# A retention kernel's chunk loop: the normalisation of a chunk is queued ahead of the next chunk's operands, and sums of background products are made by accumulating DMAs

## The chip, the cores and the metric

The kernel runs on one core of one Trainium2 chip. The metric is the device time of one execution in microseconds (us), the median over several runs. An execution is also profiled once; the profile gives its span and what each engine did in it: TensorE (PE; its weight loads are PEld), VectorE (DVE), ScalarE (ACT), GpSimd (POOL) and SyncE (SP, which here only issues DMAs).

## The reference, cut to what matters

Two layers over 1024 tokens of width 1024. Layer 0 mixes tokens by retention, layer 1 by a state-space scan; each is followed by a gated MLP. The change touches the retention of layer 0 and the modulations, which are worked out in the background of that stage:

```
def step(state, qkv):                       # one chunk of 128 tokens, per head
    qc, kc, vc = qkv
    s = jnp.einsum('bhnd,bhmd->bhnm', qc, kc) * intra[None]
    o = (jnp.einsum('bhnm,bhmv->bhnv', s, vc)
         + jnp.einsum('bhnd,bhdv->bhnv', qc, state) * cross[None, :, :, None])
    state = (chunk_decay[None, :, None, None] * state
             + jnp.einsum('bhmd,bhmv->bhdv', kc * to_state[None, :, :, None], vc))
    return state, o
...
    mu = jnp.mean(o, axis=-1, keepdims=True)
    oc = o - mu
    o = oc * lax.rsqrt(jnp.mean(oc * oc, axis=-1, keepdims=True) + EPS)
...
    mod = cond @ ada_w[i] + ada_b[i]        # cond = silu(c), shift/scale/gate of both sub-layers
```

There are 4 heads with keys of 256 and values of 512, and 8 chunks of 128 tokens. `ada_w` is 2 x 1024 x 6144; ten of its twelve blocks of 1024 x 1024 are the background's.

## The kernel before, in words

**Products.** Every fp32 operand is split into a high and a low part, and a product is three matmuls into one PSUM bank (`mm3`, L822 to L825).

**The chunk loop.** The loop over heads (L1550) computes gates, q, k and the first value tiles, and then runs over 8 chunks. The program order of one turn `ci` is: `s2(ci)`, `s1(ci+1)`, `s2_norm`, `v_tile(ci+2)`, a tick, `s3(ci)`, a tick. Each engine runs its own instructions in this order.
- `s2(ci)` puts query x state (6 matmuls, from the second chunk on) and scores x values (3 matmuls) into the bank `ob`. DVE takes its mean and variance (bn_stats L1191, bn_aggr L1193) and adds epsilon (`gve`, L1195); POOL raises that to -1/2 (`grs`, L1197). Then 6 matmuls update the state, whose fp32 form `stf` and halves `sth`, `stl` come from DVE (L1208, L1213), ACT (L1209) and, for the second half, POOL (a tensor_tensor by the helper at L128).
- `s1(ci+1)` makes the next chunk's scores, masks them (`pf`, L1156) and splits them (`pp`, L1158, L1159), transposes and splits k (`kk`, L1167 on ACT, L1168 on DVE), and splits q (`qq`, L1172 on ACT, L1173 on DVE).
- `s2_norm` makes -mean x grs (`gnb`, L1221, DVE) and the normalised chunk `on` (L1222, ACT), which reads `ob`, `grs` and `gnb`.
- `v_tile(ci+2)` is 48 matmuls of 256 columns for a later chunk's values (L1133 to L1135). For the last two chunks a gate or output unit stands in its place.
- `s3(ci)` has four PE transposes of `on` (L1229), and DVE multiplies the gates `sg` by them (L1231). Every second chunk ACT issues a DMA of `sg` to `act_d`.

**The background.** A tick pumps the queue of weight loads and takes one step of the background queue. From the first heads on that is `ada_bg` (L547): 80 steps, ten sets of eight row blocks `kt`. A step issues on SP the load of the next 512 KB block into one of two buffers `ar` (L554), multiplies the present block by its column of `cond` on POOL (L513), and adds the product to the accumulator `aacc` on POOL (L515); for kt = 0 the multiplication writes `aacc` itself. After kt = 7, `ada_fold` transposes and reduces the accumulator on DVE, with the block's buffer as scratch (L522, L523). There is one accumulator. A turn of the chunk loop has two ticks, so two steps, and they stand on POOL between the `stl` of this chunk and the `grs` of the next. The steps run through the chunk loops of heads 0 to 2 (chunks 2 to 5 of head 0, 0 to 5 of heads 1 and 2, 16 turns with two steps each) and through the units between them.

**Accumulating DMAs.** A DMA that POOL issues with `accum_op` adds its source to its destination. In the kernel before only layer 1's MLP has them (L285, L286 and L288, 256 KB each, SBUF to SBUF).

Of the kernel before, what the change touches and what calls it, by code (L numbers as in the profile page):

```python
# [12 lines left out]
F32R = mybir.dt.float32r  # L13
I32 = mybir.dt.int32
AF = mybir.ActivationFunctionType
ALU = mybir.AluOpType
PSUM = bass.MemoryType.PSUM

P = 128
# [8 lines left out]
NCH = T // CH  # L28
# [53 lines left out]
def trunk_kernel(ctx: ExitStack, tc: tile.TileContext, x, c, pos, ada_w, ada_b, ret_w_in, ret_w_out,  # L82
# [13 lines left out]
    V = nc.vector  # L96
# [33 lines left out]
    def gp_ts(out, in0, c_):  # L130
        GP.tensor_scalar(out=out, in0=in0, scalar1=c_, scalar2=1.0, op0=ALU.mult, op1=ALU.mult)
# [4 lines left out]
    def f(ap):  # L136
        return ap.bitcast(F32)
# [372 lines left out]
    def ada_acc(eng, acc, raw, kt, first):  # L510
        o = acc if first else raw
        if first or eng is GP:
            eng.tensor_scalar(out=o, in0=raw, scalar1=cond[:, kt:kt + 1], scalar2=1.0, op0=ALU.mult, op1=ALU.mult)  # L513
            if not first:
                eng.tensor_tensor(out=acc, in0=acc, in1=raw, op=ALU.add)  # L515
        else:
            eng.scalar_tensor_tensor(out=acc, in0=raw, scalar=cond[:, kt:kt + 1], in1=acc, op0=ALU.mult, op1=ALU.add)  # L517
# [29 lines left out]
    def ada_bg(order, nb):  # L547
        seq = [(l, m, kt) for l, m in order for kt in range(8)]
        raws = {}

        def load(i):
            if i < len(seq):
                raws[i] = a_p.tile([P, D], F32, tag="ar", name="ar", bufs=2)
                SP.dma_start(out=raws[i], in_=ada_slab(*seq[i]))  # L554
        load(0)
        yield
        acc = None
        for i, (l, m, kt) in enumerate(seq):
            load(i + 1)
            if kt == 0:  # L560
                acc = a_p.tile([P, D], F32, tag="aacc", name="aacc")
            raw = raws.pop(i)
            ada_acc(GP, acc, raw, kt, kt == 0)
            yield
            if kt == 7:
                ada_fold(acc, raw, l, m)
        yield
        yield from ada_fin(nb())
# [575 lines left out]
    def s1(H, ci):  # L1144
        kt, qt = qk_chunk(H.k, ci), qk_chunk(H.q, ci)
        st = bank(B_S)
        for d in range(2):
            PE.matmul(st[:, 0:P], lhsT=kt[:, d, :], rhs=qt[:, d, :], start=(d == 0), stop=(d == 1))
        r = ci % 2
        if r == 0 or ci == 0:  # L1150
            H.pf = t_p.tile([P, 2, P], F32, tag="tE", name="pf")
            H.pp = t_p.tile([P, 2, 2, P], F32R, tag="tD", name="pp")
            H.kk = t_p.tile([P, 2, 2, 256], F32R, tag="tB", name="kk")
            H.qq = t_p.tile([P, 2, 2, 2, P], F32R, tag="tC", name="qq")
        pf = H.pf[:, r, :]
        V.tensor_tensor(out=pf, in0=st[:, 0:P], in1=cst[:, C_MASK + H.h * P:C_MASK + (H.h + 1) * P], op=ALU.mult)  # L1156
        ph, pl = H.pp[:, r, 0, :], H.pp[:, r, 1, :]
        V.tensor_copy(ph, pf)  # L1158
        V.tensor_tensor(out=pl, in0=pf, in1=f(ph), op=ALU.subtract)  # L1159
        H.P[ci] = (ph, pl)  # L1160
        if ci < NCH - 1:
            kb = bank(B_KT)
            for d in range(2):
                PE.transpose(kb[:, d * P:(d + 1) * P], kt[:, d, :], ident)
            sc = cst[:, C_KS + H.h:C_KS + H.h + 1]
            kh, kl = H.kk[:, r, 0, :], H.kk[:, r, 1, :]
            A.activation(out=kh, in_=kb[:, 0:256], func=AF.Copy, scale=sc)  # L1167
            V.scalar_tensor_tensor(out=kl, in0=kb[:, 0:256], scalar=sc, in1=f(kh), op0=ALU.mult, op1=ALU.subtract)  # L1168
            H.K[ci] = (kh, kl)
        if ci > 0:  # L1170
            qh, ql = H.qq[:, r, 0], H.qq[:, r, 1]
            A.activation(out=qh, in_=qt, func=AF.Copy)  # L1172
            V.tensor_tensor(out=ql, in0=qt, in1=f(qh), op=ALU.subtract)  # L1173
            H.Q[ci] = (qh, ql)

    def s2(H, ci):
        vt = H.v[ci]
        vh, vl = vt[:, 0:512], vt[:, 512:1024]
        ob = bank(B_O)
        if ci > 0:  # L1180
            qh, ql = H.Q.pop(ci)
            for d in range(2):
                sh_, sl_ = H.st[1][:, d * HW:(d + 1) * HW], H.st[2][:, d * HW:(d + 1) * HW]
                mm3(ob, qh[:, d, :], ql[:, d, :], sh_, sl_, d == 0, False)
        ph, pl = H.P.pop(ci)
        mm3(ob, ph, pl, vh, vl, ci == 0, True)
        r = ci % 2
        if r == 0:
            H.on = t_p.tile([P, 2, HW], F32, tag="tA", name="on")
        bs = s_p.tile([P, 6], F32, tag="bs", name="bs")  # L1190
        V.bn_stats(bs, ob)  # L1191
        mv = s_p.tile([P, 2], F32, tag="mv", name="mv")
        V.bn_aggr(mv, bs)  # L1193
        ve = s_p.tile([P, 1], F32, tag="gve", name="gve")
        V.tensor_tensor(out=ve, in0=mv[:, 1:2], in1=cst[:, C_EPS + H.h:C_EPS + H.h + 1], op=ALU.add)  # L1195
        rs = s_p.tile([P, 1], F32, tag="grs", name="grs")
        GP.tensor_tensor(out=rs, in0=ve, in1=mhalf[:, 0:1], op=ALU.pow)  # L1197
        if ci < NCH - 1:
            kh, kl = H.K.pop(ci)
            sc = float(np.exp(lg[H.h] * CH))  # L1200
            for d in range(2):
                sb = bank(B_ST[d])
                mm3(sb, kh[:, d * P:(d + 1) * P], kl[:, d * P:(d + 1) * P], vh, vl, True, True)
                sf, sh_, sl_ = (t[:, d * HW:(d + 1) * HW] for t in H.st)
                if ci == 0:
                    A.activation(out=sf, in_=sb, func=AF.Copy)
                else:
                    V.scalar_tensor_tensor(out=sf, in0=sf, scalar=sc, in1=sb, op0=ALU.mult, op1=ALU.add)  # L1208
                A.activation(out=sh_, in_=sf, func=AF.Copy)  # L1209
                if d:  # L1210
                    gp_tt(sl_, sf, f(sh_), ALU.subtract)
                else:
                    V.tensor_tensor(out=sl_, in0=sf, in1=f(sh_), op=ALU.subtract)  # L1213
        drop(H.v.pop(ci))
        H.n = (ci, ob, mv, rs)
# [334 lines left out]
    for h in range(HEADS):  # L1550
        if h == 1:
            bgq.insert(0, tables_in())
        while H.ng < 4:
            g_unit(H.h, H.ng, H.sg)
            H.ng += 1
        H.q = [take(F32, f"q{i}") for i in range(2)]
        for j in range(2):
            rot_unit("q", h, j, H.q)
        H.k = [take(F32, f"k{i}") for i in range(2)]
        for j in range(2):  # L1560
            rot_unit("k", h, j, H.k)
        H.wv = W.get(("v", h, 0, 0), 4)
        H.st = (take(F32, "stf"), take(F32R, "sth"), take(F32R, "stl"))
        v_tile(H, 0)
        tick()
        s1(H, 0)
        v_tile(H, 1)
        tick()
        N = late = None
        for ci in range(NCH):  # L1570
            s2(H, ci)
            if ci + 1 < NCH:
                s1(H, ci + 1)
            if late is not None:
                s3(H, late)
                late = None
            s2_norm(H)
            if ci + 2 < NCH:
                v_tile(H, ci + 2)
                tick()  # L1580
            elif h + 1 < HEADS:
                if N is None:
                    drop(*H.q, *H.k)
                    N = new_head(h + 1)
                g_unit(N.h, N.ng, N.sg)
                N.ng += 1
            else:
                RB = Rot([0, 1, 5]) if ci < NCH - 1 else RA
                ro_unit(act, 0, ci - (NCH - 2))
            if h == HEADS - 1 and ci == NCH - 6:  # L1590
                bg_drain()
                drop(cosT, sinT, H.q.pop(0), H.k.pop(0))
                act = []
                la = load_act(0, act)
            if h == HEADS - 1 and NCH - 6 <= ci < NCH - 3:
                next(la)
            if h == HEADS - 1 and ci == NCH - 3:
                for a_, b_ in hT:
                    drop(a_, b_)
                for _ in la:  # L1600
                    pass
                xp = [take(F32, f"xp{k}") for k in range(8)]
                for k in range(8):
                    SP.dma_start(out=xp[k], in_=x_d[k])
            if h == HEADS - 1 and ci == NCH - 3:
                late = ci
            else:
                s3(H, ci)
            tick()
        drop(*H.st)  # L1610
        if N is None:
            drop(*H.q, *H.k)
        H = N
# [892 lines left out]
```

## Time and profile before

| | |
|---|---|
| median of 3 runs | 2737.92 us (2734.78 to 2738.56) |
| the profiled execution's own time | 2735.52 us |
| its span in the trace | 2733.7 us |
| mean granted TensorE clock | 0.991 of full speed |
| busy shares | PE 97%, PEld 82%, DVE 60%, ACT 31%, POOL 31% |

The profile is of one execution. In it a row of an engine's timeline gives start, duration, line, operation and tiles, and in brackets how long the engine was idle before it and what ended that. The program's names stand in the rows (`bk` is any PSUM bank).

### The profile page before, as it was taken

Reading aid. Unit: us, or ns where it says so; the run is one execution under the profiler, and the core shown is the slowest. Engines: PE = TensorE matmul, PEld = TensorE weight load, DVE = VectorE, ACT = ScalarE, POOL = GpSimd, SP = SyncE. Lnnn points to the kernel's source line nnn. Section 1 sums busy time; section 2 is a strip of 40 time slices with the busy share of each in tenths; the row PEclk is TensorE's granted clock in tenths of the full one; section 3 lists DMA queues with packets and bytes.
Section 4 is the critical chain, followed back from the end, with each engine's and each line's share of the span. In section 5 each row is a group of like instructions: output and inputs, shape, how many; then the busy total and the mean of one; then the engine's idle time right before and its main releaser. Section 6 shows DMA issues by size and latency. Waiting matters only on the chain.

```text
span 2733.7 us, 33619 instructions
## 1 busy us (share of the span) xinstructions
PE 2651.6 (97%) x13041; PEld 2228.1 (82%) x13041; DVE 1630.9 (60%) x2254; ACT 855.5 (31%) x1346; POOL 844.3 (31%) x718
## 2 busy tenths in 40 slices
PE   6999999999999999999999999999998999999999
PEld 5798888888988778888888888888876788888888
DVE  8665564655675675665556545664248666666454
ACT  5323122221321342333333223222235444343212
POOL 5345676676100433333332104221112221110004
PEclk8999999999999999999999999999999999999999
DMA  7644335343442123233223213895236966645311
GB/s 246 165 135 144 109 109 168 117 155 123 117 146 74 41 82 97 96 100 100 96 94 105 78 47 124 269 302 175 77 108 150 214 165 169 164 127 203 113 62 62
DMA packets 341821, 357.14 MB, mean 131 GB/s; under 512 B 40445, under 2 KB 279581, under 8 KB 341661
## 3 DMA queue, kind: packets, MB, share of 16 engines
q1 hardware_dynamic: 292028, 269.36, 31.9%
q10 hardware_dynamic: 36960, 62.55, 6.4%
q0 software_dynamic: 12672, 23.07, 5.0%
q8 instruction: 103, 1.69, 0.3%
q14 instruction: 58, 0.47, 0.1%
HBM read 259.82 MB, written 70.42 MB: 121 GB/s over the span
## 4 chain that ended last, share of the span: by engine, by line
PE 74%; DVE 12%; ACT 4%; DMA 4%; issue 2%; POOL 2%; SPq 0%; ACTq 0%; DVEq 0%; POOLq 0%
PE bk L823 23%; PE bk L825 23%; PE bk L824 23%; PE bk L1135 1%; PE bk L1133 1%; PE bk L1134 1%; DVE wlo L356 1%; POOL ar L128 1%; ACT whi L355 1%; DVE gve L1195 1%; DVE stf L1208 1%; DVE t L1268 1%; PE bk L1229 1%; DVE bacc L517 1%; ACT sth L1209 0%
## 5 line engine op out<-in xcount | busy, mean ns | idle before, releaser
L823 PE MATMUL bk<-hh,whi 128*128 128x512 f32 x1344 | 531.4, 395 | 7.2 <-DVE t L1683 2.5
L824 PE MATMUL bk<-hl,whi 128*128 128x512 f32 x1344 | 526.6, 392 | 5.4 <-POOL hl L128 2.6
L825 PE MATMUL bk<-hh,wlo 128*128 128x512 f32 x1344 | 526.1, 391 | 0.3 <-DVE wlo L356 0.3
L356 DVE TENSOR_TENSOR wlo<-wr,whi 128x1024 fp32r<-128x1024 f32 x173 | 243.2, 1408 | 258.9 <-ACT whi L355 258.9
L1527 DVE SCALAR_TENSOR_TENSOR x<-bk,mods,x 128x512 f32<-128x512 f32 x288 | 228.9, 813 | 189.3 <-PE bk L825 188.9
L823 PEld LDWEIGHTS bk<-hh,whi 128*128 128x128 f32 x1344 | 254.0, 189 | 63.1 <-DVE t L1683 2.9
L824 PEld LDWEIGHTS bk<-hl,whi 128*128 128x128 f32 x1344 | 254.0, 189 | 60.4 <-POOL hl L128 5.7
L825 PEld LDWEIGHTS bk<-hh,wlo 128*128 128x128 f32 x1344 | 253.8, 189 | 53.9 <-DVE wlo L356 0.7
L355 ACT ACTIVATE whi<-wr 128x1024 fp32r<-128x1024 f32 x173 | 181.2, 1055 | 271.8 <-PE bk L824 215.0
L823 PE MATMUL bk<-fh,whi 128*128 128x512 f32 (+1 forms) x608 | 232.2, 382 | 0.4 <-DVE t L1683 0.4
L824 PE MATMUL bk<-fl,whi 128*128 128x512 f32 (+1 forms) x608 | 229.9, 378 | 0.0
L825 PE MATMUL bk<-fh,wlo 128*128 128x512 f32 (+1 forms) x608 | 229.9, 378 | 0.0
L515 POOL TENSOR_TENSOR aacc<-aacc,ar 128x1024 f32<-128x1024 f32 x70 | 172.1, 2459 | 5.8
L128 POOL TENSOR_TENSOR nacc<-nacc,ar 128x512 f32<-128x512 f32 x36 | 46.6, 1294 | 411.6 <-ACT ar L633 411.4
L128 POOL TENSOR_TENSOR ar<-sp 128x512 f32<-128x512 f32 (+1 forms) x64 | 81.3, 1284 | 245.8 <-ACT sev L1459 129.1
L1133 PE MATMUL bk<-whi,hh 128*128 128x256 f32 x512 | 147.3, 288 | 0.0
L1135 PE MATMUL bk<-whi,hl 128*128 128x256 f32 x512 | 144.9, 283 | 0.0
L1134 PE MATMUL bk<-wlo,hh 128*128 128x256 f32 x512 | 144.9, 283 | 0.0
L823 PE MATMUL bk<-hs,whi 128*128 128x512 f32 x328 | 131.0, 399 | 9.2 <-DVE E L1268 6.0
L824 PE MATMUL bk<-hs,whi 128*128 128x512 f32 x328 | 130.1, 397 | 3.6 <-DVE hs L715 3.6
L823 PEld LDWEIGHTS bk<-fh,whi 128*128 128x128 f32 x608 | 114.2, 188 | 23.2 <-issue 0.8
L825 PEld LDWEIGHTS bk<-fh,wlo 128*128 128x128 f32 x608 | 114.2, 188 | 21.4
(384 smaller groups left out, 5521.9 us busy)
## 6 DMA issues: line engine op xcount, KB each, us to landing
ar<-in_ada_w SPq DMA_DIRECT2D x80, 512.0 KB, 4.4
wr<-in_ffn_w_up SPq DMA_DIRECT2D x78, 512.0 KB, 3.8
wr<-in_ret_w_in SPq DMA_DIRECT2D x48, 512.0 KB, 4.1
wr<-in_ffn_w_down SPq DMA_DIRECT2D x44, 512.0 KB, 3.3
ff_d<-t ACTq DMA_DIRECT2D x22, 512.0 KB, 4.2
fr<-ff_d SPq DMA_DIRECT2D x22, 512.0 KB, 6.1
blk<-in_ada_w SPq DMA_DIRECT2D x32, 256.0 KB, 6.0
act_d<-sg ACTq DMA_DIRECT2D x16, 512.0 KB, 5.0
```

The source lines that it names most:

```text
L128: GP.tensor_tensor(out=out, in0=in0, in1=in1, op=op)
L355: A.activation(out=hi, in_=r, func=AF.Copy)
L356: low = lambda: V.tensor_tensor(out=lo, in0=r, in1=f(hi), op=ALU.subtract)
L515: eng.tensor_tensor(out=acc, in0=acc, in1=raw, op=ALU.add)
L517: eng.scalar_tensor_tensor(out=acc, in0=raw, scalar=cond[:, kt:kt + 1], in1=acc, op0=ALU.mult, op1=ALU.add)
L823: PE.matmul(bk, lhsT=lh, rhs=rh, start=first, stop=False, skip_group_check=skip)
L824: PE.matmul(bk, lhsT=lh, rhs=rl, start=False, stop=False, skip_group_check=skip)
L825: PE.matmul(bk, lhsT=ll, rhs=rh, start=False, stop=last, skip_group_check=skip)
L1133: PE.matmul(o, lhsT=hh, rhs=wh[:, k % 4, :], start=(k == 0), stop=False)
L1134: PE.matmul(o, lhsT=hh, rhs=wl[:, k % 4, :], start=False, stop=False)
L1135: PE.matmul(o, lhsT=hl, rhs=wh[:, k % 4, :], start=False, stop=(k == 7))
L1527: V.scalar_tensor_tensor(out=dst, in0=bk, scalar=g, in1=src, op0=ALU.mult, op1=ALU.add)
```

## The change

Three edits. The line numbers behind the first lie a few higher in the changed file.
1. For kt = 1 to 6 (60 of the 80 steps) the POOL add at L515 is replaced by an accumulating DMA of 512 KB from `ar` to `aacc`, which POOL issues.
2. The split of q leaves `s1` and becomes `q_split(ci+1)`, called in `s2(ci)` between query x state and scores x values.
3. `s2_norm` is called right after `s2`, ahead of `s1(ci+1)`.

```
-            ada_acc(GP, acc, raw, kt, kt == 0)
+            if kt in (0, 7):
+                ada_acc(GP, acc, raw, kt, kt == 0)
+            else:
+                gp_ts(raw, raw, cond[:, kt:kt + 1])
+                GP.dma_start(out=acc, in_=raw, accum_op=ALU.add)
             yield
...
-            H.qq = t_p.tile([P, 2, 2, 2, P], F32R, tag="tC", name="qq")
...
-        if ci > 0:
-            qh, ql = H.qq[:, r, 0], H.qq[:, r, 1]
-            A.activation(out=qh, in_=qt, func=AF.Copy)
-            V.tensor_tensor(out=ql, in0=qt, in1=f(qh), op=ALU.subtract)
-            H.Q[ci] = (qh, ql)
+
+    def q_split(H, ci):
+        qt = qk_chunk(H.q, ci)
+        r = ci % 2
+        if r == 0 or ci == 1:
+            H.qq = t_p.tile([P, 2, 2, 2, P], F32R, tag="tC", name="qq")
+        qh, ql = H.qq[:, r, 0], H.qq[:, r, 1]
+        A.activation(out=qh, in_=qt, func=AF.Copy)
+        V.tensor_tensor(out=ql, in0=qt, in1=f(qh), op=ALU.subtract)
+        H.Q[ci] = (qh, ql)
...
+        if ci + 1 < NCH:
+            q_split(H, ci + 1)
         ph, pl = H.P.pop(ci)
...
             s2(H, ci)
+            s2_norm(H)
             if ci + 1 < NCH:
                 s1(H, ci + 1)
             if late is not None:
                 s3(H, late)
                 late = None
-            s2_norm(H)
```

On POOL, one chunk of head 0 stands so before (`stl` is the state's low half, `ar` the block's buffer, `aacc` the accumulator, `grs` the next chunk's power):

```order
L128 TENSOR_TENSOR stl<-stf,sth 128x512
L513 TENSOR_SCALAR ar<-ar,cond 128x1024
L515 TENSOR_TENSOR aacc<-aacc,ar 128x1024
L513 TENSOR_SCALAR ar<-ar,cond 128x1024
L515 TENSOR_TENSOR aacc<-aacc,ar 128x1024
L1197 TENSOR_TENSOR grs<-gve,mhalf 128x1
```

The same place on POOL after the change:

```order
L128 TENSOR_TENSOR stl<-stf,sth 128x512
L131 TENSOR_SCALAR ar<-ar,cond 128x1024
L567 DMA aacc<-ar 128x1024
L131 TENSOR_SCALAR ar<-ar,cond 128x1024
L567 DMA aacc<-ar 128x1024
L1207 TENSOR_TENSOR grs<-gve,mhalf 128x1
```

The places are the same; two adds have become two issues of a DMA. The power `grs` still stands behind both.

On DVE, the same chunk before, from the statistics of a chunk to `gnb`:

```order
L1191 BN_STATS bs<-bk 128x6
L1193 BN_AGGR mv<-bs 128x2
L1195 TENSOR_TENSOR gve<-mv,cst 128x1
L1208 SCALAR_TENSOR_TENSOR stf<-stf,bk 128x512
L1213 TENSOR_TENSOR stl<-stf,sth 128x512
L1208 SCALAR_TENSOR_TENSOR stf<-stf,bk 128x512
L1156 TENSOR_TENSOR pf<-bk,cst 128x128
L1158 CAST pp<-pf 128x128
L1159 TENSOR_TENSOR pp<-pf,pp 128x128
L1168 SCALAR_TENSOR_TENSOR kk<-bk,cst,kk 128x256
L1173 TENSOR_TENSOR qq<-q_2382,qq 128x256
L1221 SCALAR_TENSOR_TENSOR gnb<-mv,grs 128x1
```

The same stretch of DVE after the change:

```order
L1181 TENSOR_TENSOR qq<-q_2382,qq 128x256
L1201 BN_STATS bs<-bk 128x6
L1203 BN_AGGR mv<-bs 128x2
L1205 TENSOR_TENSOR gve<-mv,cst 128x1
L1218 SCALAR_TENSOR_TENSOR stf<-stf,bk 128x512
L1223 TENSOR_TENSOR stl<-stf,sth 128x512
L1218 SCALAR_TENSOR_TENSOR stf<-stf,bk 128x512
L1231 SCALAR_TENSOR_TENSOR gnb<-mv,grs 128x1
L1159 TENSOR_TENSOR pf<-bk,cst 128x128
L1161 CAST pp<-pf 128x128
L1162 TENSOR_TENSOR pp<-pf,pp 128x128
L1171 SCALAR_TENSOR_TENSOR kk<-bk,cst,kk 128x256
```

`gnb` has moved ahead of the five operations of `s1`, and the split of q ahead of the statistics. ACT's `on` and `qq` moved in the same way. The order of PE's and SP's instructions is the same in both kernels. In the changed kernel each accumulating DMA waits on POOL for the completion of the one before it, the add for kt = 7 waits for that of kt = 6, and each load at L554 waits on SP for the accumulating DMA that last read its buffer.

## Rows read from the trace of the kernel before

**Rows 1.** The page: busy us, share of the span, instructions of each engine.
```profile
PE 2651.6 (97%) x13041; PEld 2228.1 (82%) x13041; DVE 1630.9 (60%) x2254; ACT 855.5 (31%) x1346; POOL 844.3 (31%) x718
```

**Rows 2.** Waits of PE, 130 to 880 us: total us, times, longest.
```profile
PE bk L1229 <- ACT on L1222: 15.6, 12, 1.9
PE bk L825 <- DVE pp L1159: 0.3, 2, 0.2
```

**Rows 3.** Timeline of PE, one turn: start, us, operation, idle before it.
```profile
196.77 0.66 PE L1229 MATMUL bk<-cst,on 128*128 128x128 f32 x4 [1.01 <-ACT on L1222]
...
207.01 0.28 PE L1135 MATMUL bk<-whi,hl 128*128 128x256 f32 x1
208.83 0.66 PE L1229 MATMUL bk<-cst,on 128*128 128x128 f32 x4 [1.54 <-ACT on L1222]
```

**Rows 4.** Timeline of ACT in the same turn.
```profile
208.00 0.78 ACT L1222 ACTIVATE on<-bk,gnb,grs 128x512 f32<-128x512 f32 x1 [1.14 <-DVE gnb L1221]
```

**Rows 5.** Timeline of DVE in the same turn.
```profile
199.55 0.70 DVE L1191 BATCH_NORM_STATS2 bs<-bk 128x6 f32<-128x512 f32 x1 [1.03 <-PE bk L825]
...
200.50 2.39 DVE L1195 TENSOR_TENSOR gve<-mv,cst 128x1 f32<-128x1 f32 x1
...
205.45 0.28 DVE L1156 TENSOR_TENSOR pf<-bk,cst 128x128 f32<-128x128 f32 x1
...
207.76 0.14 DVE L1221 SCALAR_TENSOR_TENSOR gnb<-mv,grs 128x1 f32<-128x1 f32 x1
```

**Rows 6.** Timeline of POOL in the same turn.
```profile
200.49 2.38 POOL L515 TENSOR_TENSOR aacc<-aacc,ar 128x1024 f32<-128x1024 f32 x1
202.97 0.55 POOL L1197 TENSOR_TENSOR grs<-gve,mhalf 128x1 f32<-128x1 f32 x1
206.27 1.29 POOL L128 TENSOR_TENSOR stl<-stf,sth 128x512 fp32r<-128x512 f32 x1 [2.75 <-ACT sth L1209]
207.53 1.29 POOL L513 TENSOR_SCALAR ar<-ar,cond 128x1024 f32<-128x1024 f32 x1
```

**Rows 7.** All instructions of L1195: ns min/median/max, first and last start.
```profile
L1195 DVE TENSOR_TENSOR gve<-mv,cst x32: 158/160/2401, 158.7 to 760.2; 128x1 f32<-128x1 f32 x32
```

**Rows 8.** Groups of POOL, 160 to 690 us: busy us, mean ns, idle before.
```profile
L515 POOL TENSOR_TENSOR aacc<-aacc,ar 128x1024 f32<-128x1024 f32 x70 | 172.1, 2459 | 5.8
L513 POOL TENSOR_SCALAR ar<-ar,cond 128x1024 f32<-128x1024 f32 x70 | 96.0, 1372 | 46.2 <-DMA ar<-in_ada_w 46.2
```

**Rows 9.** Timeline of PE behind its longest wait for `on`.
```profile
511.74 1.02 PE L1229 MATMUL bk<-cst,on 128*128 128x128 f32 x4 [1.92 <-ACT on L1222]
```

**Rows 10.** Windows: length, PE busy, PEclk, DMA share, GB/s.
```profile
511.50:515.50 4.00, 3.76 (x12) 0.57 0.46 137
208.50:212.50 4.00, 3.67 (x18) 1.00 0.13 16
```

**Rows 11.** Accumulating DMAs of layer 1: two issues on POOL's timeline.
```profile
2051.59 1.44 POOL L286 DMA_DIRECT2D wr<-wra  x1
...
2055.56 0.86 POOL L288 DMA_DIRECT2D sq<-sq  x1 [2.53 <-DMA sq<-wr]
```

**Rows 12.** Window behind the second of them: length, POOL busy, PEclk, DMA share, GB/s.
```profile
2056.50:2058.50 2.00, 2.00 (x2) 1.00 0.76 131
```

**Rows 13.** Issue to landing at L288, the accumulating DMAs of 256 KB.
```profile
DMA to landing us min/median/max: 3.3/3.3/8.1
```

**Rows 14.** All loads of the background, L554, 512 KB each, issued by SP.
```profile
L554 SPq DMA_DIRECT2D ar<-in_ada_w x80: 327/328/1309, 163.5 to 675.8; - x80
...
DMA to landing us min/median/max: 3.5/4.4/6.1
```

**Rows 15.** Window around one such load, and 31 us of the loop (columns as rows 12).
```profile
363.00:366.00 3.00, 2.92 (x2) 1.00 0.54 175
351.50:382.50 31.00, 23.94 (x17) 1.00 0.40 128
```

**Rows 16.** Timeline of DVE at the end of a set of eight.
```profile
385.12 1.25 DVE L522 STREAM_TRANSPOSE ar<-aacc 128x1024 f32<-128x1024 f32 x1 [0.63 <-POOL aacc L515]
386.40 1.22 DVE L523 TENSOR_REDUCE asum<-ar 128x32 f32<-128x1024 f32 x1
```

## The prediction

> **What bounds the kernel now.** I read the page's busy shares first. PE is busy 97% of the span [rows 1], so a change that leaves PE's work and order alone can win only what PE spends waiting, or lose by new waits. The waits of PE over the chunk loops come next: twelve waits for `on` make 15.6 us, two for `pp` 0.3 [rows 2]. The rest of the loop is matmuls back to back. To see why `on` is late I followed one turn backwards. PE's last v matmul is at 207.01, the transposes start 1.54 us after it ended, at 208.83 [rows 3]. They waited for `on`, which ACT began at 208.00 after waiting for `gnb` [rows 4]. DVE ran `gnb` at 207.76, though nothing it reads was late then: POOL's `grs` was finished at 202.97 + 0.55 = 203.5 [rows 5, 6]. Between lie DVE's own queue (state, `pf`, `pp`, `kk`, `qq`), and ahead of it a tiny `gve` that took 2.39 us [rows 5], where the least is 0.158 [rows 7]. It ended 0.02 us after POOL's add at L515, which had started 0.01 us before it [rows 6]: DVE's two-input operation stood until POOL's add was over. So today two things make `on` late: DVE held for 2.39 - 0.16 = 2.23 us by the add, and `gnb` at the end of DVE's queue, where the five operations from `pf` on take 207.76 - 205.45 = 2.31 us [rows 5].
>
> One turn lasts 208.83 - 196.77 = 12.06 us, of which 1.54 is the wait [rows 3], so a turn holds 10.5 us of PE work.
>
> **What can be won.** Either edit covers the 1.54 us by itself: the reorder takes 2.31 us out of the way of `gnb`, the missing add 2.23. So both together remove the gaps, not twice as much. The gaps are 15.6 + 0.3 us [rows 2]. A long one costs more than itself: behind the longest, 1.92 us, four transposes took 1.02 us instead of 0.66 [rows 9, 3] and the granted clock was 0.57 over 4 us, so TensorE stood at its lower level (1.2 of 2.4 GHz) most of that time; behind the 1.54 us one it was 1.00 [rows 10]. That is 4 x 0.43 = 1.7 us. The ceiling is 15.9 + 1.7 = 17.6 us, and it is a ceiling for the stage, since PE's order is the same.
>
> The moved q split costs an ACT copy and a DVE subtraction ahead of the statistics instead of behind them. It is work that was there, DVE is idle 1.03 us just before the statistics [rows 5], and I cost it at nothing. If that cover were gone, DVE's half would push `on` by under 1 us, less than what `gnb` gains by its place.
>
> **What replaces the add.** POOL loses 60 adds of 2.46 us [rows 8] and gains 60 issues of 0.86 to 1.44 [rows 11]. POOL does not need the time. What counts is the wait: each accumulating DMA waits on POOL for the one before, and the next turn's `grs` is queued behind the second of a turn; who waits for `grs` is `gnb`, `on`, PE's transposes. Before, an add kept POOL for 2.4 us; now POOL stands until the last DMA has landed.
>
> No row of before shows an accumulating DMA of 512 KB. The nearest are those of 256 KB: 3.3 us from issue to landing in the median [rows 13], and the share of the 16 DMA engines in the 2 us behind one is 0.76, so 1.5 us of all engines [rows 12]. For twice the bytes I estimate 3.3 + 1.5 = 4.8 us alone, 3.0 of them with all engines busy. The block's load takes 3.5 to 6.1, median 4.4 [rows 14], alone some 4.0, and 3 x 0.54 = 1.6 us of the engines [rows 15]. Two chains then set the least time of a turn with two steps:
> - accumulate behind accumulate: 2 x 4.8 = 9.6 us;
> - a buffer's round (each of two buffers serves one step a turn): accumulate 4.8, load 4.0, multiplication 1.3 [rows 6] = 10.1 us.
>
> Alone both fit under 10.5. But one landing releases the next accumulate on POOL and the next load on SP, so the two run together. If a transfer waits out the other's whole engine time, the accumulate takes 4.8 + 1.6 = 6.4 and the load 4.0 + 1.6 = 5.6: the chains become 12.8 and 6.4 + 5.6 + 1.3 = 13.3 us. The engines would be busy 2 x 3.0 + 2 x 1.6 = 9.2 us of a turn beside other loads, where today the loop's share is 0.40 [rows 15]. So a turn's chain lies between 10.1 and 13.3; since both transfers start at the same landing, I take 12.0, above the middle.
>
> The Trainium skill says of this (DMA: Bandwidth & Descriptors, Issuing engines are not separate DMA queues) that DMAs of all issuing engines run on the same 16 engines and interleave; by that the upper sums hold, and without it the lower. The trace shows other loads landing in 3.5 to 6.1 us [rows 14], which agrees with sharing.
>
> **Slack, and where the lateness goes.** Count from the statistics' start, 199.55. PE is ready for the transposes at 208.83 - 1.54 = 207.29, so 7.74 later [rows 3]. Backwards: `on` starts 0.83 before the transposes, `gnb` 0.24 before that [rows 3 to 5], `grs` takes 0.55, handing over about 0.1: `grs` may start 6.0 us after the statistics without cost. What stands ahead of it: `stl` of the previous turn ends at 206.27 + 1.29 = 8.0 [rows 6], less the 2.23 hold 5.8; multiplication 1.3, so 7.1 for the first issue; the second half a chain later, 6.0 at 12.0 a turn; an issue 0.9: 14.0. The next statistics are 10.5 later, so `grs` is free at 3.5, and 2.5 us of slack remain. Each further turn moves it by 12.0 - 10.5 = 1.5. Each of the three heads therefore has about two free turns, and then gaps of 1.5 us: 16 turns less 6 free ones make 10 x 1.5 = 15 us. Four ends of a set lie in these turns: there the add of kt = 7 (2.4) waits for the last accumulate and the fold (1.25 + 1.22 [rows 16]) may stand ahead of the statistics; the loss beyond the steady gap I put at 0.7 each, 2.8 us. Three of these gaps would reach 1.9 us or more, with 1.7 each for the clock: 5.1. Sum 22.9, against 17.6 that go: +5.3 us. 2735.5 + 5.3 = 2740.8; the profiled execution lies 2.4 under the median of the runs, so **2743 us**.
>
> What is measurable here I take as 0.2%, 5.5 us. The forecast is thus the edge of no change: the wait of PE for `on` stays, but what it waits for is now a DMA in place of DVE's queue.
>
> **Rivals.**
> - *Accumulates keep up.* If loads and accumulates interleave with little loss, the chain is 10.1 to 10.5 and POOL's wait lies within the slack. All gaps go but about 4 us at set ends: -13.6, 2735.5 - 13.6 + 2.4 = 2724 (2721 to 2727). For it: both chains alone fit, the share would still leave 10.5 - 9.2 us, and a late accumulate spreads the two transfers out. Against: the joint release.
> - *Issues or transfers held up.* A chain of 13.2: 10 x 2.7 + 2.8, and all ten gaps long enough for the low clock, 17: 46.8 against 17.6, +29, 2767 us. A form of it that needs no contention of transfers is the issue: it took 1.44 us instead of 0.86 once [rows 11]; if each issue were held by 0.6 us by DVE's work, a turn's chain grows by 1.2, from 12.0 to 13.2, the same time. It decides from a chain of about 12 upwards; below 10.5 it costs nothing. For it: DVE's two-input operations stand while POOL computes [rows 5, 6], so the reverse could hold. Against: most issues here lie at 0.86.
> - *Nothing visible.* If the accumulate's share of the DMA engines makes it only as slow as POOL's add was late, the time is within 0.2%; that is the middle of my own forecast and not kept apart.
>
> The Trainium skill speaks for the second rival: by SBUF — State Buffer, SBUF: two separate sides, a DMA issued from POOL has its descriptors written there, and some DVE operations lock POOL out of the port pair that they share, so the transfer starts late. Rows 11 show issues between 0.86 and 1.44, so at most 0.6 us of such a hold so far.
>
> **Numbers.** Chain between 10.5 and 13, about as long as today's turn: 0.58, with times from 2732 to 2757. Accumulates keep up: 0.27. Held up: 0.15. The range goes from 2721 to 2760: it holds the first two and leaves out most of the third; the likeliest's own range is 2732 to 2757. Faster by over 0.2%: the second case and a little of the first, 0.30. Within 0.2%: half of the first, 0.28. Slower: the rest and the third, 0.42.
>
> **What the trace after would show.** Right: `gve` at 0.16 us except for a few beside kt = 7; `gnb` ahead of `pf`, but waiting for `grs`; POOL idle at the issue of the accumulating DMA, ended by the landing of the one before it, 5 to 6.5 us after that issue; in each of heads 0 to 2 gaps ahead of the transposes that begin in the third or fourth turn with steps. SP's loads start at landings. The first step of my sum to fail would be the 12.0: with accumulates landing in about 4.8 us, no gaps are left and the second case is there; from 6.4 on, gaps over 1.9 with PEclk at half behind them, the third. Wrong in another way would be gaps for `on` that end with DVE or ACT and not with POOL (the reorder does not do what its place says), waits of PE for `qq` or `kk`, which stand later or beside other work now, or waits for weights, whose loads stand on SP behind loads that wait for an accumulate.

## The result, and the profile after

The changed kernel takes 2802.81 us (median of 4 runs, 2800.03 to 2803.73) against 2738.24 us (median of 4) of the kernel before: ratio 1.0234 with a 95% interval of 1.0216 to 1.0252, 64 us slower. The range ended at 2760. The profiled execution has a span of 2801.7 us, 68.0 more than before.

The busy shares of the page come first (busy us, share of the span, instructions):

```profile
PE 2670.0 (95%) x13041; PEld 2242.0 (80%) x13041; DVE 1595.0 (57%) x2254; ACT 856.3 (31%) x1346; POOL 736.1 (26%) x718
```

PE runs the same 13041 matmuls, but is busy 18.4 us longer than in [rows 1]: the same work at a lower granted clock (0.980 of full speed on average, 0.991 before). In the other 68.0 - 18.4 = 49.6 us of the longer span PE is idle. POOL, which was to be relieved, is busy 108 us less. These are the longest waits of PE from 130 to 950 us (total, times, longest):

```profile
PE bk L1239 <- ACT on L1232: 38.2, 12, 6.3
PE bk L1082 <- DMA rows<-in_final_norm_g: 10.3, 1, 10.3
PE bk L827 <- DVE rtmp L1123: 5.9, 2, 4.7
PE bk L827 <- DVE pp L1161: 3.6, 1, 3.6
```

The waits for the normalised chunk are again twelve, as in [rows 2], and 22.6 us longer. Three kinds are new. Who made `on` late is in DVE's timeline of the turn that answers to [rows 5]:

```profile
200.10 0.69 DVE L1201 BATCH_NORM_STATS2 bs<-bk 128x6 f32<-128x512 f32 x1
...
201.04 0.16 DVE L1205 TENSOR_TENSOR gve<-mv,cst 128x1 f32<-128x1 f32 x1
...
209.38 1.22 DVE L1231 SCALAR_TENSOR_TENSOR gnb<-mv,grs 128x1 f32<-128x1 f32 x1 [5.54 <-POOL grs L1207]
210.52 0.28 DVE L1159 TENSOR_TENSOR pf<-bk,cst 128x128 f32<-128x128 f32 x1
```

`gve` takes 0.16 us and `gnb` stands ahead of `pf`, as the change says. But `gnb` waits 5.54 us for POOL's `grs`, and `pf` with the next chunk's scores waits behind it. POOL's timeline shows why:

```profile
192.62 0.89 POOL L567 DMA_DIRECT2D aacc<-ar  x1 [3.65 <-DMA aacc<-ar]
...
199.17 0.90 POOL L567 DMA_DIRECT2D aacc<-ar  x1 [1.87 <-DMA aacc<-ar]
203.56 1.11 POOL L131 TENSOR_SCALAR ar<-ar,cond 128x1024 f32<-128x1024 f32 x1 [3.49 <-DMA ar<-in_ada_w]
207.83 0.91 POOL L567 DMA_DIRECT2D aacc<-ar  x1 [3.16 <-DMA aacc<-ar]
208.43 0.92 POOL L1207 TENSOR_TENSOR grs<-gve,mhalf 128x1 f32<-128x1 f32 x1
...
214.39 0.91 POOL L567 DMA_DIRECT2D aacc<-ar  x1 [1.85 <-DMA aacc<-ar]
...
221.16 0.88 POOL L567 DMA_DIRECT2D aacc<-ar  x1 [1.85 <-DMA aacc<-ar]
```

Each issue stands until the accumulate before it has landed, and `grs` follows the second of a turn. From second issue to second issue the two turns shown take 207.83 - 192.62 = 15.2 and 221.16 - 207.83 = 13.3 us, where a turn has 10.5 us of PE work. The six other such turns, in the loops of heads 1 and 2, lie between 12.8 us (547.67 to 560.50) and 15.2 us (393.75 to 408.94); the mean of all eight is 14.1. Over the whole stage (130 to 950 us, waits of POOL, then of SP's queue):

```profile
POOL aacc L567 <- DMA aacc<-ar: 137.2, 46, 5.6
POOL ar L131 <- DMA ar<-in_ada_w: 110.7, 44, 8.1
```
```profile
SPq L554 <- DMA aacc<-ar: 406.3, 56, 16.2
```

In the kernel before, POOL did not wait at these adds for a transfer and waited 48.7 us for the block loads; SP stood at the same line for POOL's adds and multiplications, 252.8 us in all.

DVE's queue has such a place too. The fold at the end of a set reads the accumulator, so it stands until the add of kt = 7 is done, and that add waits for the last accumulate. DVE waited there for 40.2 us in eight of the ten sets; before it was 2.2 us. Two of the new waits of PE, 4.70 us for `rtmp` and 3.60 for `pp`, are for operations that stood behind such a fold in DVE's queue. These rows show the first of them, on DVE and then on PE:

```profile
698.78 1.25 DVE L522 STREAM_TRANSPOSE ar<-aacc 128x1024 f32<-128x1024 f32 x1 [8.64 <-POOL aacc L515]
```
```profile
702.53 0.79 PE L827 MATMUL bk<-hh,whi 128*128 128x512 f32 x1 [4.70 <-DVE rtmp L1123]
```

Where the time went along the program is read from PE's transposes, which stand at the same places in both kernels. These rows are the last transposes of a head's loop and the first of the next:

```profile
253.48 0.60 PE L1239 MATMUL bk<-cst,on 128*128 128x128 f32 x4
358.61 1.11 PE L1239 MATMUL bk<-cst,on 128*128 128x128 f32 x4 [5.75 <-ACT on L1232]
453.98 0.60 PE L1239 MATMUL bk<-cst,on 128*128 128x128 f32 x4
551.29 1.11 PE L1239 MATMUL bk<-cst,on 128*128 128x128 f32 x4 [3.56 <-ACT on L1232]
648.23 0.60 PE L1239 MATMUL bk<-cst,on 128*128 128x128 f32 x4
748.56 1.11 PE L1239 MATMUL bk<-cst,on 128*128 128x128 f32 x4 [6.29 <-ACT on L1232]
831.28 0.60 PE L1239 MATMUL bk<-cst,on 128*128 128x128 f32 x4
```

In the kernel before the same seven places are:

```profile
249.47 0.60 PE L1229 MATMUL bk<-cst,on 128*128 128x128 f32 x4
336.59 0.60 PE L1229 MATMUL bk<-cst,on 128*128 128x128 f32 x4
423.27 0.60 PE L1229 MATMUL bk<-cst,on 128*128 128x128 f32 x4
511.74 1.02 PE L1229 MATMUL bk<-cst,on 128*128 128x128 f32 x4 [1.92 <-ACT on L1222]
598.37 0.60 PE L1229 MATMUL bk<-cst,on 128*128 128x128 f32 x4
685.23 0.60 PE L1229 MATMUL bk<-cst,on 128*128 128x128 f32 x4
766.90 0.60 PE L1229 MATMUL bk<-cst,on 128*128 128x128 f32 x4
```

| stretch | before | after | more |
|---|---|---|---|
| up to the end of head 0 | 249.47 | 253.48 | 4.0 |
| units between heads 0 and 1, first wait included | 87.1 | 105.1 | 18.0 |
| loop of head 1 | 86.7 | 95.4 | 8.7 |
| units between heads 1 and 2 | 88.5 | 97.3 | 8.8 |
| loop of head 2 | 86.6 | 96.9 | 10.3 |
| units between heads 2 and 3 | 86.9 | 100.3 | 13.5 |
| loop of head 3 | 81.7 | 82.7 | 1.1 |

They sum to 64.4 us. The loops hold 24 of them. The units between them, in which the prediction priced nothing, hold 40. Of these 40 the new waits of PE make 34: the first `on` of a head (15.6 us, 1.9 before), the small `rows` (10.3 and 0.3), `rtmp` (5.9) and `pp` (3.6). The low clock behind five of these waits, at the prediction's 1.7 us each, would make about the rest; that is an estimate.

### The profile page after: what moved, and what is told of

It reads as the page before. It is cut to its first block, busy times and chain, and to the rows that moved or that the text cites. A ratio compares the mean times of both kernels' runs of the same rounds, so it can differ in the third digit from the quotient of the medians.

```text
span 2801.7 us, 33738 instructions
## 1 busy us (share of the span) xinstructions
PE 2670.0 (95%) x13041; PEld 2242.0 (80%) x13041; DVE 1595.0 (57%) x2254; ACT 856.3 (31%) x1346; POOL 736.1 (26%) x718
## 4 chain that ended last, share of the span: by engine, by line
PE 65%; DMA 16%; DVE 8%; issue 4%; ACT 3%; POOL 3%; SPq 1%; ACTq 0%; POOLq 0%; DVEq 0%
PE bk L827 20%; PE bk L829 20%; PE bk L828 20%; DMA aacc<-ar 11%; DMA ar<-in_ada_w 1%; POOL ar L128 1%; DMA blk<-in_ada_w 1%; DMA W<-w_d 1%; PE bk L2216 1%; PE bk L1139 1%; PE bk L1137 1%; PE bk L1138 1%; POOL ar L131 1%; DVE wlo L356 1%; ACT whi L355 0%
## 5 line engine op out<-in xcount | busy, mean ns | idle before, releaser
L356 DVE TENSOR_TENSOR wlo<-wr,whi 128x1024 fp32r<-128x1024 f32 x173 | 227.6, 1318 | 251.1 <-ACT whi L355 250.4
L828 PEld LDWEIGHTS bk<-fl,whi 128*128 128x128 f32 x608 | 114.2, 188 | 20.8
```

The source lines that it names most:

```text
L356: low = lambda: V.tensor_tensor(out=lo, in0=r, in1=f(hi), op=ALU.subtract)
L828: PE.matmul(bk, lhsT=lh, rhs=rl, start=False, stop=False, skip_group_check=skip)
```

## The experiments

Three theories stood against each other. A: POOL and SP stand in their in-order queues until an accumulating DMA has landed, and its chain sets the pace. B: the new order itself delays something. C: the added bytes on the DMA engines cost the time, whoever waits. All ratios are to the kernel before, run beside each kernel.

**The order alone** (`e1_reorder`): the changed kernel with all adds back on POOL.

```
-            if kt in (0, 7):
-                ada_acc(GP, acc, raw, kt, kt == 0)
-            else:
-                gp_ts(raw, raw, cond[:, kt:kt + 1])
-                GP.dma_start(out=acc, in_=raw, accum_op=ALU.add)
+            ada_acc(GP, acc, raw, kt, kt == 0)
```

> The order of the changed kernel (normalisation and q split moved), all adds on POOL as before. Theory A, that the loss comes from POOL and SP standing in their queues until an accumulating DMA has landed: the order alone takes PE's 15.6 us of waits for the normalised chunk away, 2715 to 2728 us. Theory B, that the moved q split or the moved normalisation delays the state or the next scores: 2745 us or more, with new waits of PE for pp, kk or sth. Theory C, that the added 31 MB on the DMA engines cost the time whoever waits: as A here.

2725.7 us, ratio 0.9969 (0.9956 to 0.9981): 0.3% faster than before. B falls as the cause of the loss. The waits of PE for `on` are three now:

```profile
PE bk L1235 <- ACT on L1228: 3.7, 3, 1.7
```

**The accumulating DMAs alone** (`e2_accum`): the diff's first edit on the kernel before, none of the others.

> The accumulating DMAs alone, in the order of before. Theory A: as the changed kernel or a little more, since the normalisation stands behind the next operands again, 2795 to 2825 us. Theory B: most of the loss is gone, 2738 to 2760. Theory C: 2795 to 2825.

2794.96 us, ratio 1.0214 (1.0196 to 1.0232). The DMAs alone make the loss. That is the lower edge of what theory A gave, which had expected as much as the changed kernel takes, or more. With the DMAs the new order does not bring its 9 us: both edits together take 2802.81 us, 1.0234. A possible reason, read from the traces and not tested, is that in the new order a late `grs` holds DVE at `gnb`, with `pf` and `pp` behind it. DVE waits there for 45.3 us in this run, and for 76.2 us in the changed kernel (130 to 960 us):

```profile
DVE gnb L1231 <- POOL grs L1207: 76.2, 20, 9.3
```

**Two accumulators** (`e4_twoacc`): even and odd blocks have each their own, so no accumulate waits for the one just before it.

```
-            if kt in (0, 7):
-                ada_acc(GP, acc, raw, kt, kt == 0)
-            else:
+            dst = (acc, acc2s[0])[kt % 2]
+            if kt < 2:
+                ada_acc(GP, dst, raw, kt, True)
+            elif kt < 7:
                 gp_ts(raw, raw, cond[:, kt:kt + 1])
-                GP.dma_start(out=acc, in_=raw, accum_op=ALU.add)
+                GP.dma_start(out=dst, in_=raw, accum_op=ALU.add)
+            else:
+                ada_acc(GP, dst, raw, kt, False)
+                GP.tensor_tensor(out=acc, in0=acc, in1=dst, op=ALU.add)
```

> The changed kernel with two accumulators, even and odd blocks, joined by one POOL add a set; kt = 1 starts the second, so 50 accumulating DMAs in place of 60. No accumulate waits for the one just before it. Theory A: POOL's 137 us of waits at the issues go, a wait for the loads stays, most of the gaps ahead of the transposes go: 2735 to 2765 us. Theory C: five sixths of the bytes are still there, 2785 us or more. Theory B: unchanged, about 2800.

2758.25 us, ratio 1.0086 (1.0073 to 1.01). As theory A said, but not all: the waits for `on` are 24.9 us, and POOL's waits for loads remain (98.9 us). With two buffers a load still waits for the accumulate of the step before.

**A third block buffer** (`e5_threebuf`): one accumulator, loads two steps ahead.

```
-                raws[i] = a_p.tile([P, D], F32, tag="ar", name="ar", bufs=2)
+                raws[i] = third[0] if i % 3 == 2 else a_p.tile([P, D], F32, tag="ar", name="ar", bufs=2)
...
+        third = [take(F32, 'ar3', newest=True)]
         load(0)
+        load(1)
...
-            load(i + 1)
+            load(i + 2)
```

> The changed kernel with a third block buffer and loads two steps ahead; all 60 accumulates still wait for one another. If the chain of accumulates behind each other is what costs (theory A): POOL's waits for loads (111 us) go, those at the issues grow, 2780 to 2800 us. If the round of a buffer (accumulate, load, multiplication) is what costs: 2740 to 2765. Theory C: 2795 to 2805.

2796.73 us, ratio 1.0228 (1.0211 to 1.0245), the same as the changed kernel within the intervals. POOL's waits for loads are gone, and those at the issues have taken their place, 233 us for the 137 us of the changed kernel:

```profile
POOL aacc L569 <- DMA aacc<-ar: 232.8, 48, 8.1
```

So with one accumulator it is the chain of accumulates that binds, not the buffers.

**Both** (`e6_both`): the two edits above together.

> The changed kernel with two accumulators and a third block buffer together (50 accumulating DMAs, loads two steps ahead): neither an accumulate nor a load waits for the accumulate just issued. Theory A, the queues that stand until an accumulate has landed: 2724 to 2735 us, the waits ahead of the transposes nearly gone. Theory C, the added traffic itself: no better than two accumulators alone, 2750 to 2765.

2730.74 us, ratio 0.998 (0.997 to 0.999). With 50 of the 60 DMAs, and no accumulate waiting for the one just issued, the loss is gone: POOL's waits at the issues fall from 137.2 to 1.9 us. A load still waits on SP for an accumulate, against the words of the expectation (181 us in all), but it is needed a step later. The loss is gone although an accumulate lands even later than in the changed kernel:

```profile
DMA to landing us min/median/max: 4.6/6.5/9.8
```

Theory C keeps the distance to the order alone, 2730.7 - 2725.7 = 5 us, and the intervals of the two ratios overlap.

**The small loads on ACT** (`e7_rows`): `tables_in`, for which PE waited 10.3 us.

```
-        SP.dma_start(out=rows2[0:66], ...
+        A.dma_start(out=rows2[0:66], ...        # and the other four alike
```

> The changed kernel with the five small loads of the MLP tables issued by ACT instead of SP, where they stand behind a block load that waits for an accumulate. If SP's queue costs its 10.3 us by itself: 2790 to 2795 us. If the chain of accumulates sets the pace of the whole stage, PE's wait of 10.3 us for these rows gives the chain time that it then needs later: 2796 to 2803.

2795.85 us, ratio 1.022 (1.0205 to 1.0235). That is 7 us less than the changed kernel, but the intervals overlap, and it is on the edge between the two expectations. PE still waits 1.2 + 6.4 us for these rows, since ACT issues the last of them at 273.40. How much of the 10.3 us SP's queue costs, and how much the chain takes back, is not settled by it.

**No background loads** (`e8_noload`): the two buffers are loaded once and multiplied again at each step; all 60 accumulates are there and wait for one another.

```
-                raws[i] = a_p.tile([P, D], F32, tag="ar", name="ar", bufs=2)
-                SP.dma_start(out=raws[i], in_=ada_slab(*seq[i]))
+                if i < 2:
+                    two.append(a_p.tile([P, D], F32, tag="ar", name="ar", bufs=2))
+                    SP.dma_start(out=two[i], in_=ada_slab(*seq[i]))
+                raws[i] = two[i % 2]
```

> The changed kernel without the background's loads: the two buffers are loaded once and multiplied again at every step, so the modulations are not the reference's. All 60 accumulates still wait for one another. If sharing the DMA engines with the block loads made the accumulates late (6.0 us in the median): they land in 4.6 to 5.2, two fit into a turn, and the time is 2720 to 2735 us. If an accumulate is that slow by itself, or by the DVE work beside its issue: still 6 us, 2780 to 2800.

2734.27 us, ratio 0.9995 (0.9985 to 1.0004). Issue to landing of the accumulates, first of this kernel, then of the changed one:

```profile
DMA to landing us min/median/max: 4.5/4.7/7.3
```
```profile
DMA to landing us min/median/max: 4.5/6.0/9.5
```

DVE's work is the same in both, so it is the sharing of the DMA engines with the block loads that makes 6.0 of 4.7. In head 0 the second issues of two turns are now 10.3 us apart (202.79 to 213.12), just under a turn's 10.5. Without the loads nearly the whole loss is gone. The run also takes the loads that wait for an accumulate out of SP's queue, so it does not tell what each of the two is worth. The issues took 0.886 to 1.056 us, against 0.883 to 1.053 in the changed kernel.

**Halved accumulates** (`e9_half`): 256 KB by DMA, the other 512 columns by a POOL add.

```
-                GP.dma_start(out=acc, in_=raw, accum_op=ALU.add)
+                GP.dma_start(out=acc[:, 0:512], in_=raw[:, 0:512], accum_op=ALU.add)
+                GP.tensor_tensor(out=acc[:, 512:1024], in0=acc[:, 512:1024], in1=raw[:, 512:1024], op=ALU.add)
```

> The changed kernel with each accumulating DMA halved to 256 KB; POOL adds the other 512 columns itself (about 1.25 us each). Theory A: landing about 4 to 4.5 us, two in a turn are 10 us or a little less, most gaps go: 2725 to 2745 us. If the fixed part of an accumulate and its wait is what costs, whatever its size: 2775 us or more.

2749.78 us, ratio 1.0048 (1.0033 to 1.0063). Landing takes 4.5 us in the median. The size counts as A says, but the time is above the expected 2745, a miss: 16.6 us of waits for `on` remain.

**The normalisation alone** (`e10_norm`): on the kernel before, `s2_norm` moved; the q split stays.

```
             s2(H, ci)
+            s2_norm(H)
             if ci + 1 < NCH:
...
-            s2_norm(H)
             if ci + 2 < NCH:
```

> The kernel before with the normalisation alone moved ahead of the next chunk's operands; the q split stays behind them, all adds on POOL. If the place of the normalisation is what the order gains: 2722 to 2730 us, waits for the normalised chunk under 5 us. If the q split has to move too: 2732 us or more.

2724.97 us, ratio 0.9966 (0.9957 to 0.9974). **The q split alone** (`e11_qsplit`): `e1_reorder` with `s2_norm` back in its old place.

> The kernel before with the q split alone moved ahead of the statistics; the normalisation stays behind the next operands, all adds on POOL. It takes 0.85 us out of DVE's queue ahead of gnb and puts it where DVE waits: gaps of about 1.5 us shrink to 0.7, 2728 to 2734 us. If it costs by delaying the statistics: 2736 or more.

2732.49 us, ratio 0.9993 (0.9983 to 1.0002). The waits for `on` shrink from 15.6 to 9.7 us, and the time is inside the expected range, but a gain is not clear of the noise. The place of the normalisation is the gain, and the q split may stand where it likes: moved with it, the time is the same within the intervals. Of the waits of PE in `e10_norm` the one for `on` is nearly gone, and a small one for the q split is new:

```profile
PE bk L825 <- DVE qq L1173: 3.6, 5, 1.8
...
PE bk L1229 <- ACT on L1222: 0.2, 1, 0.2
```

**The issue behind the power** (`e12_defer`): three buffers, and each accumulate is issued behind the next turn's `grs`, or ahead of the next step.

```
-                GP.dma_start(out=acc, in_=raw, accum_op=ALU.add)
+                pend.append((acc, raw))
...
+            flush()
             load(i + 2)
...
         GP.tensor_tensor(out=rs, in0=ve, in1=mhalf[:, 0:1], op=ALU.pow)
+        flush()
```

> The changed kernel with three block buffers, and each accumulate issued behind the next turn's power (or ahead of the next step), so that the power does not stand behind an issue that waits; all 60 accumulates still wait for one another. If the pace of the chain sets the time, whatever stands behind it: 2780 to 2800 us, the waits moved to other operands. If the place of the waiting issue ahead of the power costs: 2735 to 2760 us.

2796.04 us, ratio 1.0231 (1.0215 to 1.0247). `e5_threebuf`, which has the three buffers too, took the same time. The waits for `on` are 13.1 us, against 43.2 there and 38.2 in the changed kernel, and others came for them:

```profile
PE bk L839 <- POOL stl L128: 16.9, 7, 4.9
PE bk L1093 <- DMA rows<-in_final_norm_g: 13.3, 1, 13.3
PE bk L1251 <- ACT on L1244: 13.1, 7, 5.1
```

So the pace of the chain sets the time; what stands behind the waiting issue only decides who shows it.

## Why the prediction was wrong

The mechanism of the forecast held: the wait for `on` stayed, and what it waited for became a DMA. Its size and its extent were wrong.

- **Landing of an accumulate.** 4.8 us alone was right (4.7 in `e8_noload`). The upper bound of 6.4 beside a load is near the median of 6.0, but the longest landing took 9.5.
- **The step that failed first: a chain of 12.0 us a turn.** The eight turns measured took 12.8 to 15.2 us, 14.1 in the mean; five of them lie clearly above even my upper bound of 13.3. One landing releases both transfers, as the text said. I took a value inside the bounds because it lay "above the middle", where the joint release spoke for the end. The mechanism was the rival "held up", which I gave 0.15; and its 2767 us fell 36 us short of the result.
- **The step that cost most: counting the loops only.** The sum had 16 turns, and two free ones a head. But steps also run in the units between the loops, at every tick, and what waits there is not made up before the next loop: the first `on` of heads 1, 2 and 3 is late by 5.75, 3.56 and 6.29 us, where I expected free turns. The background is one chain from its first load to its last. In the kernel before its loads start from 163.5 to 675.8 us [rows 14], 512.3 us; after, this row says 580.1:

```profile
L554 SPq DMA_DIRECT2D ar<-in_ada_w x80: 327/328/1086, 164.3 to 744.4; - x80
```

That is 67.8 us more over 79 steps, 0.86 each, as much as the span grew (68.0). The time of the loads and the span grow together in other runs too: 59.5 and 60.4 us in `e2_accum`, 21.5 and 22.6 in `e4_twoacc`, 12.7 and 14.5 in `e9_half`. As the ticks stand at fixed places of the program, a background that runs 13% slower takes PE along, through whatever stands behind its steps in the queues of POOL, SP and DVE. A step took 7.3 us where the stage had given it 6.5. Both errors were needed for the miss: with my own 12.0 a turn, 6.0 a step, a sum over all 80 steps would have found no loss at all.
- **In the units the DMA engines are busier.** Between 255 and 283 us, ahead of head 1, their share is 0.86 (columns: length, PE busy, PEclk, DMA share, GB/s), where about the same stretch of the program had 0.46 before (the second row). The issues in the changed kernel are 9.1, 7.6 and 8.9 us apart there:

```profile
255.00:283.00 28.00, 17.41 (x75) 0.85 0.86 218
```
```profile
251.00:279.00 28.00, 28.00 (x127) 1.00 0.46 154
```
```profile
255.94 0.91 POOL L567 DMA_DIRECT2D aacc<-ar  x1 [3.33 <-DMA aacc<-ar]
...
265.08 0.88 POOL L567 DMA_DIRECT2D aacc<-ar  x1 [3.68 <-DMA aacc<-ar]
...
272.63 0.88 POOL L567 DMA_DIRECT2D aacc<-ar  x1 [3.36 <-DMA aacc<-ar]
...
281.51 0.90 POOL L567 DMA_DIRECT2D aacc<-ar  x1 [3.72 <-DMA aacc<-ar]
```

- **The ends of the sets.** I put 0.7 us on each, 2.8 in all, and had the fold only ahead of the statistics. Behind two folds PE waited 4.70 us for `rtmp` and 3.60 for `pp`.
- **SP's queue.** I named loads that stand on SP behind a waiting load, and priced them at nothing. The five small loads of `tables_in` were issued from 272.92 on, behind a block load that SP could issue only at 272.05, and PE waited 10.3 us for them, to 280.71. Before, it did not wait. Part of it is the transfer's own time, since the one that PE waited for was issued at 273.81.
- **The clock.** Its price was about right: of the twelve waits for `on` the eight from 2.91 us on were followed by transposes of up to 1.12 us instead of 0.60, and the granted clock was 0.50 to 0.62 over the 4 us behind them. With the waits of 10.3 (small loads) and 4.7 us (`rtmp`) there are ten, 17 us by my price, less the 1.7 that the kernel before had; PE's busy time grew by 18.4. The number of long waits was far off: I had put three.
- **The gain of the order** came, but smaller: 9 us in `e10_norm` and 8.7 in `e1_reorder`, where my sum took off 17.6. PE's waits for `on` do go in `e10_norm`, but 3.6 us for `qq` come for them. There was nothing to pay for the q split. That DVE was held by POOL's add was real but needed no DMA to cure: with the adds still on POOL, `on` is in time once `gnb` does not stand at the end of DVE's queue.
- **The two rules of the Trainium skill.** The Trainium skill says that DMAs of all issuing engines run on the same 16 engines and interleave (DMA: Bandwidth & Descriptors, Issuing engines are not separate DMA queues). The trace agrees: an accumulate lands in 4.7 us without the block loads and in 6.0 with them. By the Trainium skill some DVE operations keep POOL from writing the descriptors of its DMAs (SBUF — State Buffer, SBUF: two separate sides). That is not seen here: no issue took more than 1.06 us, and the landing is 4.7 us beside the same DVE work. No run here tests an operation of that kind by itself.

The fastest kernels here are `e10_norm` (2725.0) and `e1_reorder` (2725.7), which cannot be told apart.

## What to carry to other kernels

A DMA that accumulates was cheap here in engine time (an issue of 0.9 us for an add of 2.46) and long in latency (6.0 us in the median beside other loads), and the next one to the same place waited for it on the issuing engine. Before an add goes to it, multiply the number of steps by the time from issue to issue where the other transfers are densest (7.6 to 9.1 us in the units here), and compare that with the time the whole stage gives those steps (6.5 us each), not only with the places where a gap is visible now. The median landing does not do for it: 80 by 6.0 is 480 us, less than the 512 that the stage gave. Two destinations and one more buffer turned 64 us of loss into about 4 us of gain with nearly the same DMAs, and the new order with POOL's adds gained 9. And read a waiting instruction's queue to its end: on POOL the powers and state stood behind it, on DVE the next scores and whatever followed a fold, on SP small loads for something else entirely.

## What the hardware showed unexpectedly

Nearly the same traffic can be harmless or ruinous: in `e6_both` the accumulates land after 6.5 us, later than the 6.0 of the changed kernel, and the kernel is 72 us faster, since no accumulate waits for the one just issued.

The fall of the clock does not follow from the length of a wait alone. In `e9_half` a wait of 2.07 us was followed by transposes of 1.05 us, and the granted clock was 0.57 over the 4 us from 392.50 on, so TensorE stood at its lower level for most of them. In the changed kernel a wait of 3.60 us was followed by matmuls at a granted clock of 1.00 (columns of the second and fourth row as in the windows above):

```profile
392.83 1.05 PE L1240 MATMUL bk<-cst,on 128*128 128x128 f32 x4 [2.07 <-ACT on L1233]
```
```profile
392.50:396.50 4.00, 3.67 (x11) 0.57 0.40 131
```
```profile
539.00 0.47 PE L827 MATMUL bk<-v,pp 128*128 128x512 f32 x1 [3.60 <-DVE pp L1161]
```
```profile
539.00:543.00 4.00, 4.00 (x25) 1.00 0.99 345
```

The first instructions behind a wait do not show it all, either. Behind a wait of 3.20 us in `e9_half`, at 695.66, the transposes took 0.66 us, but from 696.93 on the matmuls took 0.63 us instead of 0.39, and the granted clock over the 4 us from 695.40 on was 0.67.
